# A conv stage whose TensorE instructions keep the order of the program, with tap products moved between projections, moments as column-tiled products and idle products

## The chip, the cores and the metric

The kernel runs on one core of a Trainium2 chip. The metric is the device time of one execution in microseconds (us), the median of several runs; one further execution was taken by the hardware profiler, and all rows below come from it. The engines are PE (TensorE; PEld is its weight load), DVE (VectorE), ACT (ScalarE), POOL (GpSimd) and SP (the queue that issues the DMAs). Each engine works through its own queue of instructions in order; semaphores make one wait for another.

## The reference

A decoder trunk of four layers on 256 tokens of 1024 channels. Every layer has a token mixer (latent attention, a Conformer convolution, a gated linear recurrence, attention again), a SwiGLU feed-forward part, and an embedding of its own that is gated by the residual stream. The change touches the convolution, layer 1:

```python
def _conformer_conv(u, w_pw1, b_pw1, w_dw, b_dw, ln_g, ln_b, w_pw2, b_pw2):
    a = u @ w_pw1 + b_pw1
    a = a[..., :CONV_CH] * jax.nn.sigmoid(a[..., CONV_CH:])
    a = lax.conv_general_dilated(a, w_dw[:, None, :].astype(a.dtype), window_strides=(1,),
                                 padding=[(CONV_WIDTH - 1, 0)],
                                 dimension_numbers=('NWC', 'WIO', 'NWC'),
                                 feature_group_count=CONV_CH) + b_dw
    a = jax.nn.silu(_layernorm(a, ln_g, ln_b))
    return a @ w_pw2 + b_pw2
```

That is: a projection to 2048 columns, a gate (GLU), a causal convolution of 31 taps for each of the 1024 channels by itself, a LayerNorm over the channels, silu, and an output product. Before it stands an RMSNorm of the residual, after it the residual is added.

## The kernel before, in words

All 256 tokens stay on the chip, as two tiles of 128 (the residual h); weights stream in. A large product is made of three (mm, L185): weight and activation are each split into a high and a low part, and high x high, high x low and low x high are added up in PSUM. The split of a weight is done by granule (L156): a DMA brings 128x1024 numbers (raw, 4 buffers), ACT rounds the high part (whi, 9 buffers, L167) and DVE subtracts for the low part (wlo, 8 buffers, L168).

In the conv stage channels lie on partitions, tokens on the free axis, and the 1024 channels are eight groups c of 128. Its steps, in the code's order:

- embed(1) (L387): 24 products of the layer's embedding, put into two PSUM banks ("mm") in turn, and copied to pph by ACT (L399). Then PE transposes the normed residual (hg to xT, L223).
- For each pair of groups the weights of conv_head are split, and for each group 48 products of 128x256 go to a bank of "acc" (4 buffers). ACT takes the sigmoid (L762), DVE the gated product glu (L766). For groups that are convolved on PE, tap weights tapw are loaded (L726, 2 buffers), and spread (L715) copies glu by four DMAs to four shifted windows (win, L722, 3 buffers).
- Groups 2 and 3 (CHAINS) are convolved on DVE, 31 steps each (L785, L787). The other six are convolved on PE by taps_pe (L728): 32 float32 products each, of 32 columns of weights, four of which take the four column quarters of the array.
- Groups 0 and 1 (BASE) come first. Their mean over channels (L775, weights self.mean, 1/1024 everywhere) gives base (L777), which is subtracted from all eight groups (L779, L792, L796), so that the variance can be computed as a mean of squares.
- moments (L742): for each group and token tile, co and its square (ACT, L740) are the weights of a product with two columns of self.mean, four products a group, all added up in one bank (stat) that puts the tokens on partitions. A product of ones with zeros opens that sum, another closes it (L713, L801).
- From the sums come variance, reciprocal root and mean (DVE, L803 to L808); they are put on diagonals (dg, L813) and broadcast over the partitions by PE (L814). The 24 products of embed(2) stand beside this. Then each group is normed (L822, L823), goes through silu (L824), is split and multiplied by w_pw2 (linear_rows, called at L829).

A scheduler decides in which order the instructions of one engine are issued: it takes the program's order as a start and moves instructions by the times at which it thinks their inputs are ready. issue_after and the list fence hold single instructions back. Buffers of a pool are reused in turn, so the load of a new weight waits until the split of an older one has read its buffer.

## Time and profile before

| what | time |
|---|---|
| three runs | 1421.79, 1421.91 and 1424.2 us |
| median | 1421.91 us |
| the profiled execution | 1418.08 us |
| its span (first to last instruction) | 1416.3 us |
| mean granted TensorE clock | 0.986 |

Rows of the profile are read like this. A window "A:B length, PE busy (x) ..." gives for each engine how long it worked between A and B (us from the span's start) and, in brackets, with how many instructions; then the clock that TensorE was granted (1.00 is full speed), the busy share of the DMA engines and their rate in GB/s. A row of the timeline has start, length, engine, line of the code, operation, output<-inputs, shapes and count; in square brackets, how long the engine sat idle before, and what ended that. A row of the chain of waits is one piece of the chain of work that ended last. A float32 matmul leaves two records, a matmul of fp32r numbers one. In the rows of instructions grouped by line, the last columns are busy time, mean ns of one, and idle time before them with what ended it.

### The profile page before, as it was taken

How to read it: one execution, taken by the hardware profiler on the slowest of the kernel's cores; microseconds unless marked ns; L12 is line 12 of the kernel's file. 1: busy time of each engine (PE TensorE's matmuls, PEld its weight loads, DVE VectorE, ACT ScalarE, POOL GpSimd, SP SyncE). 2: the span in 40 equal slices, each digit the busy share in tenths (PEclk: the TensorE clock that was granted, in tenths of full speed). 3: DMA queues.
4: the chain of work that ended last, by engine and by line, in shares of the span. 5: the costliest groups of instructions: out<-in, count | busy, mean ns of one | idle time of the engine just before them, and what ended most of it. 6: DMA issues, size and time to landing. Idle time of an engine off the chain costs nothing.

```text
span 1416.3 us, 20148 instructions
## 1 busy us (share of the span) xinstructions
PE 1368.3 (97%) x7269; PEld 1120.7 (79%) x7269; DVE 897.8 (63%) x1718; ACT 702.0 (50%) x1161; POOL 24.9 (2%) x55
## 2 busy tenths in 40 slices
PE   6999999998999999999999999999999999999996
PEld 6787788876976778887778887888878887788885
DVE  7866555558692965554877767555568867555556
ACT  6665444445521754443564445544445755444443
POOL 0100000000000000000000000000000100000000
PEclk9999999999897999999999999999999999999999
DMA  7523666636762466663564443755544623666632
GB/s 238 181 90 110 203 194 192 186 116 219 234 204 78 146 199 190 194 192 121 184 203 134 142 134 121 240 188 180 179 151 149 203 69 112 206 192 192 191 119 75
DMA packets 176326, 235.56 MB, mean 166 GB/s; under 512 B 11841, under 2 KB 139489, under 8 KB 176225
## 3 DMA queue, kind: packets, MB, share of 16 engines
q1 hardware_dynamic: 176224, 234.26, 52.5%
q8 instruction: 57, 0.93, 0.3%
q14 instruction: 45, 0.36, 0.1%
HBM read 229.68 MB, written 1.05 MB: 163 GB/s over the span
## 4 chain that ended last, share of the span: by engine, by line
PE 73%; DMA 9%; DVE 9%; ACT 5%; issue 3%; SPq 0%; DVEq 0%; ACTq 0%
PE mm L188 13%; PE mm L189 13%; PE mm L190 13%; PE acc L189 7%; PE acc L188 7%; PE acc L190 7%; DVE wlo L168 4%; DMA raw<-in_ffn_w_down_dram 4%; PE tr L223 3%; ACT whi L167 3%; DMA raw<-in_ple_w_gate_dram 2%; DVE co L787 1%; PE mm L732 1%; PE acc L949 1%; PE acc L619 1%
## 5 line engine op out<-in xcount | busy, mean ns | idle before, releaser
L168 DVE TENSOR_TENSOR wlo<-raw,whi 128x1024 fp32r<-128x1024 f32 (+2 forms) x420 | 498.8, 1201 | 153.5 <-ACT whi L167 110.5
L167 ACT ACTIVATE whi<-raw 128x1024 fp32r<-128x1024 f32 (+2 forms) x420 | 427.9, 1040 | 273.4 <-DMA raw<-in_ffn_w_down_dram 95.8
L188 PE MATMUL mm<-whi,xT 128*128 128x512 f32 x816 | 328.4, 402 | 0.7 <-ACT xT L210 0.4
L189 PE MATMUL mm<-wlo,xT 128*128 128x512 f32 x816 | 321.6, 394 | 0.0
L190 PE MATMUL mm<-whi,xT 128*128 128x512 f32 x816 | 321.5, 394 | 0.0
L190 PEld LDWEIGHTS mm<-whi,xT 128*128 128x128 f32 x816 | 153.3, 188 | 32.6 <-DVE xT L211 0.8
L188 PEld LDWEIGHTS mm<-whi,xT 128*128 128x128 f32 x816 | 153.5, 188 | 30.5 <-ACT xT L210 0.9
L189 PEld LDWEIGHTS mm<-wlo,xT 128*128 128x128 f32 x816 | 153.7, 188 | 28.4
L188 PE MATMUL acc<-whi,aT 128*128 128x512 f32 x352 | 138.6, 394 | 0.3
L189 PE MATMUL acc<-wlo,aT 128*128 128x512 f32 x352 | 138.7, 394 | 0.0
L190 PE MATMUL acc<-whi,aT 128*128 128x512 f32 x352 | 136.4, 389 | 0.0
L337 DVE SCALAR_TENSOR_TENSOR ga<-mm,rs_y,sg 128x256 f32<-128x256 f32 x88 | 42.4, 481 | 142.9 <-ACT sg L335 142.9
L335 ACT ACTIVATE sg<-mm,rs_y 128x256 f32<-128x256 f32 x88 | 40.9, 465 | 139.3 <-PE mm L190 139.2
L188 PE MATMUL acc<-whi,xT 128*128 128x512 f32 (+2 forms) x272 | 102.5, 379 | 1.4 <-ACT whi L167 0.8
L190 PE MATMUL acc<-whi,xT 128*128 128x512 f32 (+2 forms) x272 | 102.9, 380 | 0.2 <-DVE xT L211 0.2
L189 PE MATMUL acc<-wlo,xT 128*128 128x512 f32 (+2 forms) x272 | 102.5, 378 | 0.0
L188 PEld LDWEIGHTS acc<-whi,aT 128*128 128x128 f32 x352 | 66.1, 188 | 17.1 <-ACT aT L210 2.8
L190 PEld LDWEIGHTS acc<-whi,aT 128*128 128x128 f32 x352 | 66.1, 188 | 15.8 <-DVE aT L211 1.0
L189 PEld LDWEIGHTS acc<-wlo,aT 128*128 128x128 f32 x352 | 66.2, 188 | 13.0
L211 DVE TENSOR_TENSOR aT<-tr,aT 128x256 fp32r<-128x256 f32 x88 | 37.3, 423 | 53.3 <-ACT aT L210 53.3
L188 PEld LDWEIGHTS acc<-whi,xT 128*128 128x128 f32 x272 | 51.1, 189 | 10.3 <-ACT xT L210 1.3
L190 PEld LDWEIGHTS acc<-whi,xT 128*128 128x128 f32 x272 | 51.2, 188 | 8.3 <-DVE xT L211 0.8
(256 smaller groups left out, 1804.6 us busy)
## 6 DMA issues: line engine op xcount, KB each, us to landing
raw<-in_ffn_w_gu_dram SPq DMA_DIRECT2D x352, 256.0 KB, 4.4
raw<-in_ffn_w_down_dram SPq DMA_DIRECT2D x88, 512.0 KB, 4.4
raw<-in_ple_w_gate_dram SPq DMA_DIRECT2D x32, 512.0 KB, 4.9
raw<-in_hgrn_w_in_dram SPq DMA_DIRECT2D x64, 256.0 KB, 3.8
raw<-in_mla_w_out_dram SPq DMA_DIRECT2D x16, 512.0 KB, 4.2
raw<-in_conv_w_pw_dram SPq DMA_DIRECT2D x32, 256.0 KB, 5.0
raw<-in_mla_w_in_dram SPq DMA_DIRECT2D x16, 336.0 KB, 4.0
raw<-in_mla_w_uq_dram SPq DMA_DIRECT2D x12, 384.0 KB, 4.0
```

Of the source, the lines that this page charges most:

```text
L167: nc.scalar.activation(hi[:, :used], raw[:, :used], AF.Copy)
L168: nc.vector.tensor_tensor(out=lo[:, :used], in0=raw[:, :used], in1=hi[:, :used].bitcast(F32), op=ALU.subtract)
L188: mm(ps, x[0], w[0], start=start, stop=False)
L189: mm(ps, x[0], w[1], start=False, stop=False)
L190: return mm(ps, x[1], w[0], start=False, stop=stop)
L211: v = self.nc.vector.tensor_tensor(out=lo, in0=src, in1=hi.bitcast(F32), op=ALU.subtract)
L223: nc.tensor.transpose(pt[:, (i - k0) * P : (i - k0 + 1) * P], src[:, i * P : (i + 1) * P], self.ident)
L335: nc.scalar.activation(sg, ps[:, :256], AF.Silu, scale=r)
L337: nc.vector.scalar_tensor_tensor(out=ga, in0=ps[:, 256:], scalar=r, in1=sg, op0=ALU.mult, op1=ALU.mult)
L619: nc.tensor.matmul(s1[:, hh], qT[:HD, h, P:], kT[:HD, h], start=True, stop=False)
L732: nc.tensor.matmul(ps[32 * j : 32 * j + 32], tapw[c][:, j, m], win[c][:, j, QUAD * m : QUAD * m + S], start=m == 0, stop=m == STEPS - 1,)
L787: V.scalar_tensor_tensor(out=co[:, c], in0=xin[c][:, k : k + S], scalar=par(c, k), in1=co[:, c], op0=ALU.mult, op1=ALU.add)
```

## The change

It rewrites the conv stage's order and three of its steps. While self.pinned is set, every matmul that goes through the new helper is issued in the order of the program. Groups 0 and 1 are now those convolved on DVE, their chains begin behind the gate of group 2 and advance six taps with each further group; groups 2 and 3 make the base. The taps of a group follow the projection that is two groups later, and load the tap weights of the group after next when they are issued. The moments are column-tiled: for each pair of groups four products with 32 columns of self.mean as weights and co or its square, 256 tokens, as moving input, one for each column quarter; the sums lie on four rows, are copied to SBUF, and two products with a matrix select put them on the tokens' partitions. embed(1) takes the four banks of "acc"; behind it come 12 bf16 products that nobody reads. The buffers called "work" go from five to three, and the squares have four of their own ("sq").

```diff
+    def matmul(self, *args, **kw):
+
+        ins = self.nc.tensor.matmul(*args, **kw)
+        if self.pinned:
+            self.tc.keep_in_program_order(ins)
+        return ins
...
-        mm = self.nc.tensor.matmul
+        mm = self.matmul
...
+    def idle(self, n):
+
+        ps = self.bank("mm", 2)[:, :S]
+        for _ in range(n):
+            self.matmul(ps, self.ident_bf, self.causal.rearrange("p h n -> p (h n)"), start=True, stop=True)
+
+    def embed(self, i, bank=None):
...
-                ps = self.bank("mm", 2)
+                ps = bank() if bank else self.bank("mm", 2)
...
+        self.select = C.tile([P, 2], F32, name="select")
+        nc.gpsimd.memset(self.select, 0.0)
+        for j in range(QUAD):
+            nc.gpsimd.memset(self.select[32 * j : 32 * j + 1, j % 2 : j % 2 + 1], 1.0)
...
-        BASE = 2
-        CHAINS = (2, 3)
+        CHAINS, BASE = (0, 1), (2, 3)
...
-            self.embed(i)
+            self.embed(i, self.acc)
+            self.idle(12)
...
-            zero = tmp("zero", [P, 4 * NT], 1)
-            nc.gpsimd.memset(zero, 0.0)
-            stat = self.bank("tr", 2)
-            nc.tensor.matmul(stat[:, : 4 * NT], self.ones, zero, start=True, stop=False)
-            xin, win, tapw, sq = [], {}, {}, {}
+            xin, win, tapw, sq = {}, {}, {}, {}
...
-                        nc.tensor.matmul(
+                        self.matmul(
...
-                return ps
+                if c + 2 < KD:
+                    tap_weights(c + 2)
+                if c in BASE:
+                    nc.scalar.activation(co[:, c], ps, AF.Identity, bias=par(c, TAPS))
+                else:
+                    V.scalar_tensor_tensor(out=co[:, c], in0=ps, scalar=par(c, TAPS), in1=self.base, op0=ALU.add, op1=ALU.subtract)
+                    square(c)
 
             def square(c):
-                sq[c] = tmp("work", [P, S], 5)
-                return nc.scalar.activation(sq[c], co[:, c], AF.Square)
...
+                sq[c] = tmp("sq", [P, S], 4)
+                self.sq = nc.scalar.activation(sq[c], co[:, c], AF.Square)
+
+            stats = []
+
+            def moments(pair, last=False):
+
+                if not stats:
+                    stats.append(self.bank("tr", 2)[:, :S])
+                first = len(stats) == 1
+                stats.append(pair)
+                for q, c in enumerate(pair):
+                    for m, x in enumerate((co[:, c], sq[c])):
+                        j = 2 * q + m
+                        ins = self.matmul(stats[0][32 * j : 32 * j + 32], self.mean[:, :32], x, start=first, stop=last)
+                return ins
...
+            def chain(c, k0, k1):
+                for k in range(k0, k1):
...
+            def set_base():
+
+                pm = self.bank("tr", 2)[:, :S]
+                for b in BASE:
+                    self.matmul(pm, self.mean, co[:, b], start=b == BASE[0], stop=b == BASE[-1])
+                self.base = tmp("base", [P, S], 1)
+                V.tensor_scalar(out=self.base, in0=pm, scalar1=KD / len(BASE), scalar2=None, op0=ALU.mult)
+                for c in BASE:
+                    V.tensor_tensor(out=co[:, c], in0=co[:, c], in1=self.base, op=ALU.subtract)
+                    square(c)
+
+            self.pinned = True
+            for c in (2, 3):
+                tap_weights(c)
+            for c in range(KD):
...
+                if c not in CHAINS:
+                    spread(c)
+                if c == 4:
+                    taps_pe(2)
+                if c == 5:
+                    taps_pe(3)
+                if c == 6:
+                    set_base()
+                    taps_pe(4)
+                if c >= 2:
+                    k = min(TAPS, 6 * (c - 1))
+                    for b in CHAINS:
+                        chain(b, 6 * (c - 2), k)
+            taps_pe(5)
+            moments(BASE)
             self.embed_weights(2)
             rows = lambda k: self.granule([(a["conv_w_pw2"][0][k * P : (k + 1) * P], 0)], 1, D)
             ws = [rows(k) for k in range(5)]
-            for c in CHAINS:
-                V.tensor_tensor(out=co[:, c], in0=co[:, c], in1=base, op=ALU.subtract)
-                square(c)
-                moments(c)
-            for c in range(4, KD):
-                V.scalar_tensor_tensor(out=co[:, c], in0=taps_pe(c), scalar=par(c, TAPS), in1=base, op0=ALU.add, op1=ALU.subtract)
-                fence = [square(c).ins]
-                fence.append(moments(c).ins)
+            taps_pe(6)
+            moments((4, 5))
+            for b in CHAINS:
+                V.tensor_tensor(out=co[:, b], in0=co[:, b], in1=self.base, op=ALU.subtract)
+                square(b)
+            taps_pe(7)
+            fence = [self.sq.ins]
+            moments(CHAINS)
+            fence.append(moments((6, 7), True).ins)
...
-            nc.tensor.matmul(stat[:, : 4 * NT], self.ones, zero, start=False, stop=True)
+            sums = tmp("sq", [P, S], 4)
+            V.tensor_copy(sums, stats[0])
+            tok = self.bank("tr", 2)
+            for t in range(NT):
+                self.matmul(tok[:, 2 * t : 2 * t + 2], sums[:, t * P : (t + 1) * P], self.select, start=True, stop=True)
             st = tmp("st", [P, 2, NT], 1)
-            V.tensor_copy(st, stat[:, : 4 * NT].rearrange("p (m t two) -> p m t two", m=2, two=2)[:, :, :, 0])
+            V.tensor_copy(st, tok[:, : 2 * NT].rearrange("p (t m) -> p m t", m=2))
...
+            self.pinned = False
```

The order in which the instructions are issued changes at three places on which much of the stage hangs. In the rows, a number behind a name tells one buffer's use from another's; xN stands for N like rows in a line.

TensorE, in the stage's end. Before, here is where the taps of group 4 (mm_4257) and the moments of groups 0 to 2 are (tr_3478 is the bank of the sums, work the squares):

```order
L732 MATMUL mm_4257<-win_3827,tapw_3770 32x256 x17
L748 MATMUL tr_3478<-mean,co_3475 128x2
L732 MATMUL mm_4257<-win_3827,tapw_3770 32x256 x8
L748 MATMUL tr_3478<-mean,work_4120 128x2
L748 MATMUL tr_3478<-mean,co_3475 128x2
L748 MATMUL tr_3478<-mean,work_4120 128x2
L748 MATMUL tr_3478<-mean,co_3475 128x2
L732 MATMUL mm_4257<-win_3827,tapw_3770 32x256 x4
L748 MATMUL tr_3478<-mean,work_4127 128x2
L748 MATMUL tr_3478<-mean,co_3475 128x2
L748 MATMUL tr_3478<-mean,work_4127 128x2
L748 MATMUL tr_3478<-mean,co_3475 128x2
```

After, this is all from the last product of group 7's projection (acc_4174) to group 7's taps (mm_4373; mm_4236 are those of group 5, mm_4327 of group 6, tr_4274 the bank of the sums):

```order
L188 MATMUL acc_4174<-xT_3248,wlo_4047 128x256
L188 MATMUL mm_4236<-win_3972,tapw_4010 32x256 x32
L188 MATMUL tr_4274<-co_3494,mean 32x256
L188 MATMUL tr_4274<-sq_4119,mean 32x256
L188 MATMUL tr_4274<-co_3494,mean 32x256
L188 MATMUL tr_4274<-sq_4122,mean 32x256
L188 MATMUL mm_4327<-win_4108,tapw_4157 32x256 x32
L188 MATMUL tr_4274<-co_3494,mean 32x256
L188 MATMUL tr_4274<-sq_4160,mean 32x256
L188 MATMUL tr_4274<-co_3494,mean 32x256
L188 MATMUL tr_4274<-sq_4272,mean 32x256
L188 MATMUL mm_4373<-win_4229,tapw_4269 32x256 x32
```

The moments stand in fours between whole groups of taps, where they were strewn among them one by one; group 7's taps have nothing but moments, statistics and embedding products behind them.

The queue SP, from group 6's to group 7's windows. Before (win_4047 and win_4109 are those of groups 6 and 7, tapw_3990 and tapw_4052 their tap weights):

```order
L722 DMA win_4047<-glu_4043 128x1x284 x4
L164 DMA raw_4233<-in_conv_w_pw_dram 128x1024
L164 DMA raw_4239<-in_conv_w_pw_dram 128x1024
L164 DMA raw_4512<-in_conv_w_pw_dram 128x1024
L164 DMA raw_4530<-in_conv_w_pw_dram 128x1024
L726 DMA tapw_3990<-in_conv_taps_dram 128x1024
L722 DMA win_4109<-glu_4105 128x1x284 x4
L726 DMA tapw_4052<-in_conv_taps_dram 128x1024
L164 DMA raw_4548<-in_conv_w_pw_dram 128x1024
L164 DMA raw_4691<-in_ffn_w_gu_dram 128x2x256 x2
```

After (win_4108 and win_4229 are those of groups 6 and 7, tapw_4157 and tapw_4269 their tap weights):

```order
L736 DMA win_4108<-glu_4104 128x1x284 x4
L165 DMA raw_4323<-in_conv_w_pw_dram 128x1024
L740 DMA tapw_4157<-in_conv_taps_dram 128x1024
L165 DMA raw_4516<-in_conv_w_pw_dram 128x1024
L165 DMA raw_4534<-in_conv_w_pw_dram 128x1024
L165 DMA raw_4552<-in_conv_w_pw_dram 128x1024
L736 DMA win_4229<-glu_4225 128x1x284 x4
L740 DMA tapw_4269<-in_conv_taps_dram 128x1024
L165 DMA raw_4695<-in_ffn_w_gu_dram 128x2x256 x2
```

Tap weights of a group now stand behind taps that ran before, and four loads of 128x1024 stand between the windows of group 6 and those of group 7.

VectorE, between the gates of groups 6 and 7. Before (glu_4043 and glu_4105 are those gates):

```order
L766 SCALAR_TENSOR_TENSOR glu_4043<-acc_3992,cb_1806,work_4041 128x256
L787 SCALAR_TENSOR_TENSOR co_3475<-glu_3738,cpar,co_3475 128x256
L168 TENSOR_TENSOR wlo_4208<-raw_4209,whi_4207 128x1024
L787 SCALAR_TENSOR_TENSOR co_3475<-glu_3738,cpar,co_3475 128x256
L168 TENSOR_TENSOR wlo_4214<-raw_4215,whi_4213 128x1024
L168 TENSOR_TENSOR wlo_4220<-raw_4221,whi_4219 128x1024
L168 TENSOR_TENSOR wlo_4226<-raw_4227,whi_4225 128x1024
L766 SCALAR_TENSOR_TENSOR glu_4105<-acc_4054,cb_1806,work_4103 128x256
L777 TENSOR_SCALAR base_4117<-tr_4114 128x256
L779 TENSOR_TENSOR co_3475<-co_3475,base_4117 128x256 x2
```

After (glu_4104 and glu_4225 are those gates; base_4116 is the base):

```order
L809 SCALAR_TENSOR_TENSOR glu_4104<-acc_4053,cb_1806,work_4102 128x256
L789 TENSOR_SCALAR base_4116<-tr_4113 128x256
L791 TENSOR_TENSOR co_3494<-co_3494,base_4116 128x256 x2
L169 TENSOR_TENSOR wlo_4304<-raw_4305,whi_4303 128x1024
L831 TENSOR_TENSOR co_3494<-co_3494,base_4116 128x256 x2
L755 SCALAR_TENSOR_TENSOR co_3494<-mm_4124,cpar,base_4116 128x256
L169 TENSOR_TENSOR wlo_4310<-raw_4311,whi_4309 128x1024
L169 TENSOR_TENSOR wlo_4316<-raw_4317,whi_4315 128x1024
L169 TENSOR_TENSOR wlo_4322<-raw_4323,whi_4321 128x1024
L809 SCALAR_TENSOR_TENSOR glu_4225<-acc_4174,cb_1806,work_4223 128x256
L755 SCALAR_TENSOR_TENSOR co_3494<-mm_4236,cpar,base_4116 128x256
```

Four low parts of weights, the base and the subtractions stand between the two gates, and the last three low parts right ahead of group 7's.

More of the change, by code (lines that the diff above doesn't have):

```diff
@@ L735, in taps_pe @@
                         )
-                return ps
-            def square(c):
-                sq[c] = tmp("work", [P, S], 5)
-                return nc.scalar.activation(sq[c], co[:, c], AF.Square)
-            def moments(c):
-                for t in range(NT):
-                    s = slice(t * P, (t + 1) * P)
-                    for m, x in enumerate((co[:, c, s], sq[c][:, s])):
-                        at = 2 * (NT * m + t)
-                        last = nc.tensor.matmul(stat[:, at : at + 2], x, self.mean[:, :2], start=False, stop=False)
-                return last
@@ L751, in conv @@
-            for c0 in range(0, KD, 2):
-                ws = self.conv_head(i, c0) if c0 else self.head
-                for cc in range(2):
-                    c = c0 + cc
-                    if c not in CHAINS:
-                        tap_weights(c)
-                    ps = self.acc()
-                    for half in range(2):
-                        s = slice(half * 256 + cc * P, half * 256 + (cc + 1) * P)
-                        self.mms(ps[:, half * S : (half + 1) * S], [(hi[:, s], lo[:, s]) for hi, lo in ws], xs)
-                    sg = tmp("work", [P, S], 5)
-                    nc.scalar.activation(sg, ps[:, S:], AF.Sigmoid, bias=self.cb1[:, KD + c : KD + c + 1])
-                    x = tmp("glu", [P, PAD + S + 2], 4)
-                    nc.gpsimd.memset(x[:, :PAD], 0.0)
-                    nc.gpsimd.memset(x[:, PAD + S :], 0.0)
-                    V.scalar_tensor_tensor(out=x[:, PAD : PAD + S], in0=ps[:, :S], scalar=self.cb1[:, c : c + 1], in1=sg, op0=ALU.add, op1=ALU.mult)
-                    xin.append(x)
-                    if c not in CHAINS:
-                        spread(c)
-                if c0 == 4:
-                    for c in range(BASE):
-                        nc.scalar.activation(co[:, c], taps_pe(c), AF.Identity, bias=par(c, TAPS))
@@ L787, in conv @@
                         V.scalar_tensor_tensor(out=co[:, c], in0=xin[c][:, k : k + S], scalar=par(c, k), in1=co[:, c], op0=ALU.mult, op1=ALU.add)
+            def set_base():
[11 more added lines that the diff above has]
+            for c in range(KD):
+                if c % 2 == 0:
+                    ws = self.conv_head(i, c) if c else self.head
+                ps = self.acc()
+                for half in range(2):
+                    s = slice(half * 256 + c % 2 * P, half * 256 + (c % 2 + 1) * P)
+                    self.mms(ps[:, half * S : (half + 1) * S], [(hi[:, s], lo[:, s]) for hi, lo in ws], xs)
+                sg = tmp("work", [P, S], 3)
+                nc.scalar.activation(sg, ps[:, S:], AF.Sigmoid, bias=self.cb1[:, KD + c : KD + c + 1])
+                x = xin[c] = tmp("glu", [P, PAD + S + 2], 4)
+                nc.gpsimd.memset(x[:, :PAD], 0.0)
+                nc.gpsimd.memset(x[:, PAD + S :], 0.0)
+                V.scalar_tensor_tensor(out=x[:, PAD : PAD + S], in0=ps[:, :S], scalar=self.cb1[:, c : c + 1], in1=sg, op0=ALU.add, op1=ALU.mult)
+                if c not in CHAINS:
[13 more added lines that the diff above has]
+            moments(BASE)
             self.embed_weights(2)
@@ L814, in conv @@
                     nc.tensor.matmul(bc[:, m, t], self.ones, dg, start=True, stop=True)
+            self.pinned = False
             self.fence = fence + [last.ins]
@@ L820, in conv @@
             for c in range(KD):
-                z = tmp("work", [P, S], 5)
+                z = tmp("work", [P, S], 3)
                 V.tensor_tensor(out=z, in0=co[:, c], in1=rb, op=ALU.mult)
```

12 lines of the change are left out of this document (removed).

## The prediction

> **What bounds the kernel now.** I read the page first, its busy times and its row of the granted clock in 40 slices.
>
> ```profile
> PE 1368.3 (97%) x7269; PEld 1120.7 (79%) x7269; DVE 897.8 (63%) x1718; ACT 702.0 (50%) x1161; POOL 24.9 (2%) x55
> ```
>
> ```profile
> PEclk9999999999897999999999999999999999999999
> ```
>
> TensorE is busy for 97% of the span (1416.3 us), so time goes only where its work shrinks, its clock rises or a wait of its own ends. The clock row dips in slices 11 and 13 (354 to 389 us and 425 to 460 us), which is the conv stage, all that the change touches. So I cut that stage by granted clock in the view of windows.
>
> ```profile
> core 0: us, PE busy (x) PEld busy (x) DVE busy (x) ACT busy (x) POOL busy (x), PEclk, DMA share, GB/s
> 354.84:365.08 10.24, 8.44 (x36) 7.30 (x35) 8.49 (x12) 5.78 (x8) 2.35 (x1) 0.50 0.79 247
> 365.08:423.11 58.03, 54.91 (x546) 49.77 (x544) 45.97 (x90) 20.58 (x27) 0.62 (x8) 1.00 0.70 210
> 423.11:440.17 17.06, 17.02 (x112) 11.40 (x110) 2.84 (x3) 2.72 (x7) 0.00 (x0) 0.50 0.33 105
> 440.17:453.83 13.66, 12.61 (x175) 7.83 (x168) 1.78 (x6) 2.74 (x5) 0.00 (x0) 1.00 0.34 118
> 453.83:457.24 3.41, 3.41 (x10) 2.67 (x9) 2.71 (x17) 0.60 (x1) 0.00 (x0) 0.50 0.00 0
> ```
>
> The projections run at full clock. Then come 17.06 us in which taps and moments are computed at half clock, and 3.41 us more at the stage's end. The timeline of PE shows what stands ahead of the first (idle time and its releaser in brackets); the chain of waits (start, length, what) shows what runs inside it and after it.
>
> ```profile
> 421.96 0.38 PE L748 MATMUL tr<-mean,co 128*128 128x2 f32 x2 [3.12 <-DVE co L779]
> ```
>
> ```profile
> 423.49 1.87 PE tr L748 x8
> ...
> 442.72 0.76 PE tr L748 x6
> ```
>
> A float32 product leaves two records (the tap row below has 128 for the 64 products of two groups), so a moment product takes 0.47 us there (four in 1.87) and 0.25 at full clock (three in 0.76). The sum below forecasts the start of the first product of linear_rows, which ends the stage (461.94 us, with the tail's rows below). What follows it is left alone, and its weights lie ready: from 453.83 on no DMA runs.
>
> **The change part by part.** At 365.08 the clock is full and group 0 half projected. What PE does from there I add up anew, from windows of PE alone over the two stretches of projections, and a window of the tap products alone, which lies between them.
>
> ```profile
> 365.08:396.87 31.79, 31.79 (x266) 1.00 0.77 230
> 403.92:415.66 11.74, 11.74 (x101) 1.00 0.53 142
> ```
>
> ```profile
> 396.87:403.92 7.05, 7.05 (x128) 4.06 (x128) 1.00 0.41 111
> ```
>
> The projections are the same 384 products in both kernels; those left at 365.08 take 31.79 + 11.74 = 43.5 us. Taps are computed on PE for six groups in both; two take 7.05, so six 21.2 us (0.11 us for each column-tiled product of 256 tokens). Of the moments, 32 products of two columns (32 x 0.25 = 8.0 us at full clock, twice that at half) become 16 of the shape of a tap product. I take a tap product's time, 16 x 0.11 = 1.8 us. The lower end can't be under that, since each streams the same 256 columns; the upper is a 128-wide float32 product of 256 tokens, the mean sum in this row of the timeline (four records, two products, 1.02 us, so 0.5 us each and 8.0 in all), should the four not run beside each other.
>
> ```profile
> 415.54 1.02 PE L775 MATMUL tr<-co,mean 128*128 128x256 f32 x4
> ```
>
> The mean sum keeps its 1.0 us and moves ahead of the taps of group 4. Its wait for the activation of group 3's taps is hidden by the 5.8 us of group 6's projection (48 x 0.12). The sum is 365.1 + 43.5 + 21.2 + 1.8 + 1.0 = 432.6 us, if PE never waits. Counted back from there, group 6 is projected at 410.0, group 7 at 420.2, and group 7's taps are due at 428.2 (432.6 less 3.5 of taps and 0.9 of moments).
>
> The wait that is added is that for group 7's last transfers. Its windows and tap weights are the last loads of the stage, and PE, whose order is now fixed, can't do anything else meanwhile: behind these taps stand eight moment products, the statistics and the output product.
>
> ```profile
> 413.70 2.64 SPq L722 DMA_DIRECT2D win<-glu  x4
> ```
>
> ```profile
> raw<-in_conv_w_pw_dram SPq DMA_DIRECT2D x6, 512.0 KB, 5.7
> ```
>
> ```profile
> DMA to landing us min/median/max: 3.8/4.3/7.4
> ```
>
> ```profile
> 419.36 0.47 ACT work L762
> ...
> 420.63 0.48 DVE glu L766
> ```
>
> These are the issue of a group's windows on SP (timeline), the landing of the weight loads around it (issues from 411 to 428 us), that of the tap weights, and group 7's sigmoid and glu in the chain. In the new order group 7's glu stands on VectorE behind three low parts of weights, the last one's load behind group 6's windows. Group 6 projected at 410.0, sigmoid and glu 1.0, four window issues 2.6, landing of the load 5.7, its high part 1.0 and low part 1.2 (means of the page's rows below): 421.5. That is later than the sigmoid of group 7 itself (420.7). With glu 0.5, its window issues 2.6 and the tap weights behind them on the same queue (4.3 to land), it is 428.9 when they are there, 0.7 after PE is due; with the longest landing, 7.4, 3.8 after. As three loads of 512 KB stand right ahead on the queue, I take about the middle, 2.4 us, and keep both ends.
>
> The 24 products of embed(1), now with four banks, no longer wait for pph, which the second of these pieces shows:
>
> ```profile
> 346.60 0.40 PE L188 MATMUL mm<-whi,pT 128*128 128x512 f32 x1
> 346.84 0.40 PE L189 MATMUL mm<-wlo,pT 128*128 128x512 f32 x1
> ```
>
> ```profile
> 353.60 0.51 PE L188 MATMUL mm<-whi,pT 128*128 128x512 f32 x1 [1.97 <-ACT pph L399]
> ...
> 357.29 1.08 PE L223 MATMUL tr<-ident,hg 128*128 128x128 f32 x4 [1.77 <-DVE hg L78]
> ```
>
> At 0.23 us apart they end at 346.6 + 24 x 0.23 = 352.1. The 12 that nobody reads cost 12 x 0.11 = 1.3 us at a tap product's rate for 256 columns (0.5 each and 6 us if they went like the mean sum) and end at 353.4. The transposes wait for hg, that is VectorE and the loads, until 357.29. So both change nothing; without that cover the idle products would cost their 1.3 us.
>
> What drops the clock stands in three more windows; the piece of the chain behind them is a projection product at half clock.
>
> ```profile
> 351.42:354.84 3.42, 1.45 (x6) 1.05 (x6) 1.86 (x5) 2.83 (x4) 0.00 (x0) 1.00 1.01 337
> 419.69:423.11 3.42, 1.15 (x18) 0.71 (x18) 3.18 (x7) 1.17 (x3) 0.00 (x0) 1.00 0.98 335
> 730.30:733.70 3.40, 1.64 (x10) 1.13 (x9) 2.18 (x3) 3.35 (x6) 0.00 (x0) 1.00 0.97 307
> ```
>
> ```profile
> 364.06 0.21 PE acc L190
> ```
>
> After 3.4 us with 42% and 34% of PE busy it was halved, with 48% not. The pause before the transposes, 353.4 to 357.3, still leaves a stretch of that kind, so I keep the half clock up to 365.08 as it was. [...] I charge one stretch at half clock, 3.4 / 2 = 1.7 us; the ends are 0 and 3.4.
>
> [...]
>
> The tail, from the last moment product to linear_rows, is in the chain of waits
>
> ```profile
> 453.40 0.33 PE mm L188
> ...
> 461.94 0.50 PE acc L188
> ```
>
> ```profile
> 421.03 0.41 DVE L777 TENSOR_SCALAR base<-tr 128x256 f32<-128x256 f32 x1
> ```
>
> 461.94 - 453.40 = 8.5 us, by way of VectorE's statistics. There come on top the copy of the sums (0.4, as base in the second row), two select products (0.25 each, the two-column rate) and up to three embedding products ahead of them (0.3 by what they outlast the copy): 9.7 us. At full clock the embedding products among the chain leave up to 1.0 less than this, since the broadcasts stand behind them; should the added products come at half clock, their 0.8 doubles.
>
> On VectorE the chains of groups 0 and 1 now begin with group 2, ahead of low parts of weights. From its timeline:
>
> ```profile
> 370.65 0.48 DVE L766 SCALAR_TENSOR_TENSOR glu<-acc,cb,work 128x256 f32<-128x256 f32 x1 [5.18 <-ACT work L762]
> ...
> 398.70 12.37 DVE L787 SCALAR_TENSOR_TENSOR co<-glu,cpar,co 128x256 f32<-128x256 f32 x31
> ```
>
> ```profile
> L168 DVE TENSOR_TENSOR wlo<-raw,whi 128x1024 fp32r<-128x1024 f32 (+2 forms) x420 | 498.8, 1201 | 153.5 <-ACT whi L167 110.5
> L167 ACT ACTIVATE whi<-raw 128x1024 fp32r<-128x1024 f32 (+2 forms) x420 | 427.9, 1040 | 273.4 <-DMA raw<-in_ffn_w_down_dram 95.8
> ```
>
> Between the first glu and the last low part for groups 6 and 7 stand 48 chain steps (0.40 each), five glu (0.48) and eight low parts (1.2): 370.7 + 19.2 + 2.4 + 9.6 = 401.9. Group 6's first products come at 404.2 (410.0 less 5.8), so this costs nothing with 2.3 us in hand. The 31 taps on two groups are the same work as before; fewer "work" and more "sq" buffers, the other memsets and the subtraction of base from other groups change neither count nor path. Tap weights for groups 4 to 6 are issued over 10 us before their use, against 4.3 to land.
>
> **Sum.** 432.6 + 2.4 + 1.7 + 9.7 = 446.4 against 461.9: 15.5 us less. The profiled execution took 1418.08 us (1.8 around its span), so 1402.6; the median of the runs, 1421.91, is 3.8 above it, and I carry the difference over to it: 1406.4. As a check by what goes: the wait of 3.1, half of 17.1, the moments' 6.2 and some 1.5 us of small waits are 19.3; 2.4, 1.7 and 1.2 come back, which leaves 14.0.
>
> **The rivals.** The clock holds (chance 0.15): a wait short of 1.9 us doesn't halve it, and the idle products fill enough of the pause before the transposes. Then 1.7 goes, the wait is nearer 0.7 (1.7), and at the start 24 projection products take 0.12 in place of 0.21 us (2.2 more): 1401 us. [...] The moments don't run side by side (0.08), so that the change does not do what it says there: 16 x 0.5 in place of 1.8 adds 6.2: 1412.6. Against it stands the tap row, the same tiling. VectorE comes late (0.17): it runs in order, so a chain step that waits for a glu, or a low part that waits for its load, holds all behind it, group 7's glu last. In the old kernel that glu came at 420.63, 5.0 us after the projections' end (415.66), held up by a low part. It costs nothing up to 2.3 us of delay and then one for one. Up to 12.7 us beyond it the change is still faster (0.08, some 1412); to 18.3 it can't be told from none (0.05, about 1422). Only from 18 us on, where nearly every low part waits for a load of 5.7 us and three such waits add up, is it slower (0.04): some 1427.
>
> **How the numbers follow.** The forecast has 0.60. Its own range comes from the wait (0.7 to 3.8), the clock (0 to 3.4) and the tail (8.7 to 10.5): 1402 to 1410. The range is 1399.5 to 1414, down to the held clock with the short tail, up to the untiled moments and the mild lateness. A measurement of this kernel can tell about 0.2%, 2.8 us. Faster by more: 0.60 + 0.15 + 0.08 + 0.08 = 0.91; within: 0.05; slower: 0.04.
>
> **What would show it.** In the new profile the first product of linear_rows starts near 446 us, and PE goes from group 7's projection to its taps with 1 to 4 us of idle before them and nowhere else. The granted clock is 1.00 from 365 to about 428 us, and the moment products take 0.11 us. The forecast is wrong if the projections wait for low parts (groups 4 to 7 longer than 5.8 us each), if a clock of 0.50 shows earlier, or if a stage after linear_rows waits where it did not.

## The result, and the profile after

The changed kernel takes 1401.65 us in the median of four runs (1400.18 to 1402.87), the kernel before 1421.85 in the median of its four by then (1419.49 to 1424.2): 20.2 us less, a ratio of 0.9846 with a 95% interval of 0.9821 to 0.987. The profiled execution of the changed kernel took 1402.87 us.

The page of the profile after, its span, busy times and clock:

```profile
span 1400.9 us, 20099 instructions
...
PE 1351.1 (96%) x7249; PEld 1109.8 (79%) x7249; DVE 898.1 (64%) x1719; ACT 700.4 (50%) x1161; POOL 26.2 (2%) x59
...
PEclk9999999999999999999999999999999999999998
```

VectorE and ScalarE do the same work as before, TensorE is busy for 17 us less, and the dip of the clock in slices 11 and 13 is gone. The windows of the conv stage, cut by granted clock and with the columns of before, show what is left of it:

```profile
359.39:362.80 3.41, 3.29 (x15) 3.03 (x15) 2.06 (x3) 2.85 (x4) 2.37 (x1) 0.50 0.78 255
362.80:431.07 68.27, 65.28 (x720) 56.28 (x722) 52.98 (x98) 26.39 (x37) 0.70 (x8) 1.00 0.77 240
431.07:434.48 3.41, 3.41 (x36) 2.16 (x39) 0.00 (x0) 0.00 (x0) 0.00 (x0) 0.50 0.13 44
434.48:446.68 12.20, 11.07 (x89) 7.60 (x81) 6.70 (x29) 5.14 (x10) 0.00 (x0) 1.00 0.01 1
```

6.8 us at half clock, where there were 30.7 (10.24 + 17.06 + 3.41). From group 7's projection on, the timeline of PE has two waits, one of 2.99 us ahead of group 7's taps and one of 0.99 ahead of linear_rows; the chain of waits shows what ends the first:

```profile
420.02 3.66 PE L188 MATMUL mm<-win,tapw 128*32 128x256 f32 x64
430.99 5.35 PE L188 MATMUL mm<-win,tapw 128*32 128x256 f32 x64 [2.99 <-DMA tapw<-in_conv_taps_dram]
446.68 0.50 PE L188 MATMUL acc<-whi,xT 128*128 128x512 f32 x1 [0.99 <-ACT xT L218]
```

```profile
420.79 0.04 ACT whi L168
...
421.75 0.47 ACT work L805
...
423.02 0.49 DVE glu L809
...
426.13 0.02 SPq L740
...
426.18 4.68 DMA tapw<-in_conv_taps_dram
430.85 0.14 issue
430.99 5.35 PE mm L188 x64
436.33 1.66 PE tr L188 x16
```

Group 7's sigmoid (L805) comes behind a high part of weights (L168), its glu at 423.02, then its windows, then its tap weights, and PE stands still from 428.0 to 431.0. Linear_rows starts at 446.68, and from there to the end it is 954.2 us, as before (954.4).

Executions of one kernel differ in layer 0 already: the transposes of layer 0's gate start at 331.18 us in the first profile of the changed kernel and at 329.27 in its second. So stages are compared from here on by one stretch, from the transposes of layer 0's gate (329.96 in the first row, before; 331.18 after) to the first product of linear_rows:

```profile
329.96 1.23 PE L223 MATMUL tr<-ident,hg 128*128 128x128 f32 x8 [0.97 <-DVE hg L69]
```

```profile
331.18 1.23 PE L231 MATMUL tr<-ident,hg 128*128 128x128 f32 x8 [1.72 <-DVE hg L69]
```

It fell from 132.0 us (461.94 - 329.96) to 115.5. The table has it for every run, read from the same two rows of each trace, with the longest wait of PE between the last projection and the last taps, and the time at half clock in the stage's two ends. The kernel before had medians of 1420.9 to 1422.1 us beside these runs, which were made on more than one chip. Two slow executions are left out of the medians and ratios: one of tapw7_early (2229.09 us at a granted clock of 0.557) and one of before beside all_idle22 (1676.74 us at 0.75).

| run | median us | ratio to before (95%) | stretch us | wait us | half clock at the start, at the end, us |
|---|---|---|---|---|---|
| before, 1st profile | 1421.85 | | 132.0 | 3.1 | 10.2, 20.5 |
| before_2 (2nd profile) | | | 131.8 | 3.1 | 6.8, 20.5 |
| changed | 1401.65 | 0.9846 (0.9821 to 0.987) | 115.5 | 3.0 | 3.4, 3.4 |
| same | 1400.49 | 0.9846 (0.9818 to 0.9874) | 113.9 | 2.5 | 3.4, 0 |
| unpinned | 1401.6 | 0.9851 (0.9822 to 0.988) | 115.7 | 3.4 | 3.4, 3.4 |
| old_moments | 1404.13 | 0.9869 (0.9845 to 0.9894) | 118.0 | 0 | 3.4, 6.8 |
| before_tiled | 1406.97 | 0.9895 (0.9867 to 0.9923) | 118.7 | 4.4 | 0, 6.8 |
| before_early | 1415.09 | 0.9962 (0.9944 to 0.998) | 128.0 | 2.2 | 0, 17.1 |
| idle0 | 1404.03 | 0.9882 (0.9851 to 0.9913) | 113.4 | 1.7 | 6.8, 0 |
| idle40 | 1404.16 | 0.9881 (0.985 to 0.9912) | 116.8 | 3.7 | 0, 6.8 |
| early_glu | 1400.12 | 0.9848 (0.9821 to 0.9874) | 114.0 | 2.4 | 6.8, 0 |
| tapw7 | 1397.86 | 0.9845 (0.9816 to 0.9875) | 111.6 | 0.5 | 3.4, 0 |
| tapw7_early | 1394.98 | 0.9823 (0.9794 to 0.9852) | 110.8 | 0 | 3.4, 0 |
| all_idle22 | 1397.76 | 0.9841 (0.9821 to 0.9862) | 110.9 | 0 | 3.4, 0 |

### The profile page after: what moved, and what is told of

It is laid out like the page before. It is cut to its first block, busy times and chain, and to the rows that moved or that the text cites. A ratio compares the mean times of both kernels' runs of the same rounds, so it can differ in the third digit from the quotient of the medians.

```text
span 1400.9 us, 20099 instructions
## 1 busy us (share of the span) xinstructions
PE 1351.1 (96%) x7249; PEld 1109.8 (79%) x7249; DVE 898.1 (64%) x1719; ACT 700.4 (50%) x1161; POOL 26.2 (2%) x59
## 4 chain that ended last, share of the span: by engine, by line
PE 78%; DMA 8%; DVE 6%; ACT 5%; issue 3%; SPq 1%; DVEq 0%; ACTq 0%
PE mm L188 42%; PE acc L188 25%; PE tr L231 4%; ACT whi L168 2%; DVE wlo L169 2%; DMA raw<-in_ffn_w_down_dram 2%; DMA raw<-in_ple_w_gate_dram 2%; DMA raw<-in_mla_w_ukv_dram 1%; PE acc L992 1%; PE acc L633 1%; DMA raw<-in_conv_w_pw_dram 1%; DMA raw<-in_hgrn_w_in_dram 1%; PE tr L614 1%; PE tr L654 1%; PE acc L659 1%
## 5 line engine op out<-in xcount | busy, mean ns | idle before, releaser
L168 ACT ACTIVATE whi<-raw 128x1024 fp32r<-128x1024 f32 (+2 forms) x420 | 427.8, 1040 | 265.3 <-DMA raw<-in_ffn_w_down_dram 99.2
L188 PE MATMUL mm<-whi,xT 128*128 128x512 f32 x1632 | 546.7, 398 | 0.8 <-ACT xT L218 0.4
L188 PE MATMUL acc<-whi,aT 128*128 128x512 f32 x704 | 232.9, 392 | 0.7 <-DVE aT L219 0.6
L188 PE MATMUL acc<-whi,xT 128*128 128x512 f32 (+2 forms) x544 | 165.4, 380 | 1.7 <-ACT xT L218 1.4
L218 ACT ACTIVATE xT<-tr 128x512 fp32r<-128x512 f32 (+1 forms) x72 | 37.5, 526 | 40.5 <-PE tr L231 39.7
L188 PEld LDWEIGHTS acc<-wlo,xT 128*128 128x128 f32 x272 | 51.5, 190 | 7.8
L188 PE MATMUL mm<-whi,cT 128*128 128x384 f32 (+1 forms) x160 | 52.3, 382 | 4.4 <-ACT q L602 4.1
L218 ACT ACTIVATE aT<-tr 128x256 fp32r<-128x256 f32 x88 | 33.0, 375 | 46.2 <-PE tr L231 46.0
L231 PE MATMUL tr<-ident,hg 128*128 128x128 f32 x192 | 31.2, 288 | 22.6 <-DVE hg L69 16.5
L70 ACT ACTIVATE junk<-h 128x512 bf16<-128x512 f32 x48 | 30.0, 626 | 45.1 <-DVE h L320 25.7
```

The costliest lines, as they stand in the source:

```text
L70: square = nc.scalar.activation(T.tmp("junk", [P, 512], 1, BF16), h[:, s], AF.Square, accum_out=ss[:, c : c + 1])
L168: nc.scalar.activation(hi[:, :used], raw[:, :used], AF.Copy)
L188: ins = self.nc.tensor.matmul(*args, **kw)
L218: a = self.nc.scalar.activation(hi, src, AF.Copy)
L231: nc.tensor.transpose(pt[:, (i - k0) * P : (i - k0 + 1) * P], src[:, i * P : (i + 1) * P], self.ident)
```

## Experiments: what the gain is made of

**same** is the changed kernel once more.

> The changed kernel again, as a measure for the runs beside it. The sum of the prediction gives 15 to 16 us less than before (ratio 0.989); the runs so far gave 20 us (0.985). If the sum holds, more runs come nearer to 0.989 and a profile again shows the first product of linear_rows near 446.5 us; if something outside the conv stage also gained, the ratio stays at 0.985 and some later stage is shorter than before.

Its median is 21.6 us under that of before, its profile has the stretch at 113.9 us: 1.6 less than the first profile, with no half clock behind a wait of 2.5 us. The first product of linear_rows started at 443.1. So the part that was expected of the sum alone (a ratio of 0.989) didn't come, and no later stage is shorter either: 954.5 us from linear_rows on.

**before_2** is the kernel before, for a second profile.

> The kernel before once more, for a second profile. Its first profile was of an execution 4 us under its median (1418.1 against 1422), that of the changed kernel at its median, and that is the difference between the 15 us of the sum and the 20 us of the medians. If the excess lies in the conv stage: the stretch from the gate's transposes of layer 0 (329.96 us in the first profile) to the first product of linear_rows (461.94) is longer than 132.0 us here, with more stretches at half clock or a longer wait for group 7's glu, by about what the time is above 1418. If it lies elsewhere: 132 us again, whatever the time.

It took 1418.02 us, and the stretch is 131.8 us with the same wait and the same 17.1 us at half clock. Both profiled executions of before so took 1418 us, where the medians of its runs lie at 1421 to 1422 and single ones between 1414 and 1429. The traces show 16 to 18 us of gain in the stage; where the 3 to 4 us are by which the medians lie above them, no trace shows.

**old_moments** puts back the old moments, and nothing else:

```diff
-                        ins = self.matmul(stats[0][32 * j : 32 * j + 32], self.mean[:, :32], x, start=first, stop=last)
+                            ins = self.matmul(stats[0][:, at : at + 2], x, self.mean[:, :2], start=False, stop=False)
...
-            V.tensor_copy(sums, stats[0])
...
-                self.matmul(tok[:, 2 * t : 2 * t + 2], sums[:, t * P : (t + 1) * P], self.select, start=True, stop=True)
+            self.matmul(stats[0][:, : 4 * NT], self.ones, zero, start=False, stop=True)
```

> The changed kernel with the moments as before (four products of two columns for each group, opened and closed by the products of ones and zeros), at the changed places. Theory of the sum: 32 x 0.25 in place of 16 x 0.11 us adds 6.2, the copy and the two select products go (1.2): 5 us slower than the changed kernel, up to 8 if the last sixteen fall into the half clock. Rival, that the new places of the taps carry the gain and the moments lie beside other work: within 1 us of the changed kernel.

2.5 to 3.6 us slower than the changed kernel's two medians; the stretch is 2.5 to 4.1 us longer. That lies between the two theories, as each had left out one thing. The moments do take longer, but group 7's loads arrive meanwhile: PE doesn't wait at all. And what they cost is paid in the clock, in these windows of PE's last taps, the last sixteen moments (from 434.0 on) and the tail:

```profile
430.20:433.59 3.39, 3.28 (x61) 2.39 (x65) 0.00 (x0) 0.00 (x0) 0.00 (x0) 1.00 0.11 39
433.59:437.00 3.41, 3.41 (x39) 3.00 (x28) 0.48 (x1) 1.90 (x3) 0.00 (x0) 1.00 0.02 5
437.00:443.83 6.83, 6.83 (x21) 5.70 (x21) 3.02 (x19) 0.60 (x1) 0.00 (x0) 0.50 0.00 0
```

In the second window PE is busy for every one of its 3.41 us, and yet the clock is halved behind it. All but its first 0.4 us is filled with products of two columns.

**before_tiled** is the other half alone: the kernel before with the new moments, copy and select products (moments by pairs; diff as above, the other way round).

> The kernel before with the column-tiled moments, copy and select products alone; places of the taps, chains, base and embedding as before. Theory of the sum: the half clock behind the late glu stays, 20 moments at 0.47 and 12 at 0.25 us (12.4) become 16 at up to 0.22 (3.5), 1.2 come back in the tail and about 1 in a wait for the last tap weights: 6 to 8 us faster than before. Rival (the new places carry it): 0 to 2 us faster.

15.1 us faster than before, twice what was expected, and neither theory gave it. The stretch is 13.3 us shorter, though the late glu of group 7 still makes PE wait, even longer than before (4.4 us against 3.1). Up to 2.9 of the 13.3 us are luck at the stage's start, of which the edit touches only the one product that opened the old sum: the clock was not halved there this time (nor in before_early, which leaves that product), and the last product of the projections starts 82.5 us behind the gate's transposes, where it started 85.5 us behind them in the first profile of before and 85.3 in the second. From there on the stage is 10.4 us shorter. Windows ahead of, within and behind its half clock:

```profile
415.26:418.67 3.41, 1.29 (x21) 0.48 (x10) 2.29 (x3) 1.82 (x3) 0.00 (x0) 1.00 0.88 290
418.67:425.50 6.83, 4.43 (x34) 1.77 (x36) 5.37 (x9) 3.34 (x7) 0.00 (x0) 0.50 0.86 307
425.50:438.81 13.31, 13.09 (x220) 8.61 (x214) 1.69 (x4) 1.25 (x3) 0.00 (x0) 1.00 0.60 195
```

Here too a half clock comes with the wait (416.6 to 420.9 us), but it ends after 6.83 us; with two-column products among the taps it took 17.06 us, PE busy for 17.02 of them. The second dip, in the tail, is gone too. The expectation had charged only the moments' own time, and had kept the half clock.

**before_early** was to take most of the wait out of the kernel before, and leaves its moments:

```diff
+            self.fence = [gate.ins, glu.ins]
             ws = [rows(k) for k in range(5)]
+            self.fence = []
```

(gate and glu are group 7's sigmoid and glu; behind the fence stand the high and low parts of w_pw2.)

> The kernel before with the splits of w_pw2's weights held behind group 7's sigmoid and glu; moments and places as before. This takes most of the 3.1 us wait away but leaves the two-column moments. If these count little for the clock (in the run with the old moments at the changed places it fell at 437.0 with no wait ahead of it): the 17 us at half clock stay, or come elsewhere among the moments, and it is 2 to 5 us faster than before. If the wait alone brings the half clock: 3.1 + 8.5, that is 10 to 12 us faster.

5.8 us faster in the medians, the stretch 4.0 us shorter. Again up to 2.7 us of that are luck, as the clock was not halved at the start; from the last product of the projections on the stage is 1.3 us shorter. The wait itself only fell from 3.1 to 2.2 us, since chain steps and low parts on VectorE still stand ahead of group 7's glu and the base, and PE was busy for 35% of the stretch in which it lies. So this run does not show what the kernel before would do without the wait. The time at half clock at the stage's end is again 17.1 us, now in two pieces; ahead of the second PE was busy for 82% of a stretch (2.80 of 3.40 us):

```profile
414.20:417.60 3.40, 1.18 (x12) 0.46 (x10) 3.37 (x7) 1.81 (x3) 0.00 (x0) 1.00 0.89 246
417.60:427.80 10.20, 10.20 (x82) 6.04 (x82) 6.50 (x8) 4.21 (x7) 0.00 (x0) 0.50 0.66 215
431.30:434.70 3.40, 2.80 (x28) 1.76 (x27) 0.48 (x1) 0.42 (x1) 0.00 (x0) 1.00 0.10 11
434.70:441.50 6.80, 6.80 (x56) 3.66 (x58) 0.00 (x0) 0.00 (x0) 0.00 (x0) 0.50 0.92 316
```

Ahead of the second piece PE had waited for 0.6 us only, so the reading that the wait alone brings the half clock doesn't hold for this piece. Nor does the busy share of PE tell where it comes: the clock was halved behind stretches of about 3.4 us with 0% (idle0, below), 34%, 42% and 79% (before), 63% (all_idle22, below) and 100% of PE busy (old_moments), and not behind one with 48% (before, the prediction's third row). What halves it these runs don't show. Nor does a run tell what it is about the old moments: they differ from the new ones in the two moving columns and in the 128 columns of weights that each of them loads. The row of before with 79%, ahead of the half clock of 3.41 us at its stage's end, is

```profile
450.41:453.83 3.42, 2.70 (x27) 1.95 (x20) 0.81 (x4) 1.90 (x3) 0.00 (x0) 1.00 0.00 0
```

New moments alone give 13.3 us of the stretch, the new places alone 14.0 (old_moments against before), both together 16.5 to 18.1, each with some luck at the start in it. Either one alone takes the half clock at the stage's end from 20.5 to 6.8 us, so that they don't add up.

**unpinned** leaves the order to the scheduler:

```diff
-            self.pinned = True
+            self.pinned = False
```

> The changed kernel with the scheduler left free to order TensorE's instructions. One product of group 1's projection moves ahead by 45 places, some chain steps of VectorE trade places; nothing else does. If the gain comes from the order in which the code is written: as the changed kernel, within 0.2%. If holding the scheduler to it matters (the one product waits for a bank, or the chain steps hold up low parts): 1 to 3 us slower.

1401.6 us against 1401.65 and 1400.49, the stretch 115.7. The order comes from the place of the lines in the code; holding the scheduler to it changes nothing that can be measured.

## Experiments: the products nobody reads, and the wait that is left

**idle0** drops the call, **idle40** has 40 in place of 12.

```diff
-            self.idle(12)
```

> The changed kernel without the 12 products that nobody reads. Prediction's step (they lie beside the wait for VectorE and change nothing): within 1 us of the changed kernel. Rival (they keep the clock up): in all profiles of the changed kernel the clock was halved for one stretch of 3.4 us around the transposes, in the one of before for three; without them it is two or three again, 1.7 to 3.4 us slower, with a window of 0.50 from about 354 us on.

> The changed kernel with 40 such products in place of 12: they last 4.6 to 5.0 us and fill the wait of 3.5 to 3.8 us before the transposes nearly whole. If the clock follows how much PE does in a stretch of 3.4 us: no 0.50 around 360 us, the transposes and a dozen projection products at full clock, 1 to 2 us faster than the changed kernel. If they change nothing, as the prediction has it for the twelve: within 0.5 us. If they run past the wait: up to 1 us slower.

Without them the clock is halved for 6.82 us at the transposes in place of 3.41, behind a window in which PE did nothing:

```profile
352.65:356.06 3.41, 0.00 (x0) 0.00 (x0) 2.92 (x6) 2.79 (x5) 0.00 (x0) 1.00 0.71 240
356.06:362.88 6.82, 5.48 (x23) 4.98 (x24) 5.10 (x8) 4.25 (x6) 2.36 (x1) 0.50 0.84 253
```

Yet the stretch is 113.4 us, no longer than in any run of the changed kernel: the last product of the projections starts 0.3 to 0.9 us later than in the changed kernel's two profiles, and the wait before group 7's taps is 1.7 us in place of 2.5 and 3.0. With 40, 18 of which the scheduler put between and behind the transposes, the start has no half clock at all, and the projections end 1.0 to 1.5 us sooner, yet the stretch is 116.8: a wait of 3.7 us comes ahead of group 6's taps. On VectorE a low part of weights whose load landed late now stands ahead of group 6's glu, which comes at 417.46 us, where in the changed kernel it came at 411.71; so group 6's windows and tap weights are issued late. First the changed kernel, then the one with 40:

```profile
411.71 0.47 DVE L809 SCALAR_TENSOR_TENSOR glu<-acc,cb,work 128x256 f32<-128x256 f32 x1
```

```profile
416.31 1.23 DVE L169 TENSOR_TENSOR wlo<-raw,whi 128x1024 fp32r<-128x1024 f32 x1 [3.31 <-ACT whi L168]
417.46 0.48 DVE L809 SCALAR_TENSOR_TENSOR glu<-acc,cb,work 128x256 f32<-128x256 f32 x1
```

The medians of both are 2.4 to 3.7 us above those of the changed kernel, with intervals that overlap. So the traces show no worth in the twelve, and the medians don't exclude 3 us.

**early_glu** holds the splits of the last three weights behind group 7's gate, by a fence as in before_early.

> The changed kernel with the splits of the last three weights (high part on ScalarE, low part on VectorE) held behind group 7's sigmoid and glu. Theory: the wait of 3.0 us before group 7's taps comes from these splits, whose loads land late; the glu then comes near 421 in place of 423.0 us, the wait falls to 0.5 to 1.5 us, and the half clock behind it goes too: 1.5 to 4 us faster. Rival: the tap weights' landing alone ends the wait (their buffer comes free with group 5's taps): at most 0.7 us faster.

1400.12 us: no gain that can be told. Group 7's windows were issued from 420.73 on, 2.8 us sooner than in the changed kernel (1.5 sooner by the start of the stretch), and PE waited 2.4 us all the same. The queue SP, in the changed kernel and then here:

```profile
423.56 2.51 SPq L736 DMA_DIRECT2D win<-glu  x4
426.18 1.10 SPq L740 DMA_DIRECT2D tapw<-in_conv_taps_dram  x1
```

```profile
420.73 2.50 SPq L736 DMA_DIRECT2D win<-glu  x4
423.33 0.55 SPq L165 DMA_DIRECT2D raw<-in_conv_w_pw_dram  x1
423.97 0.42 SPq L740 DMA_DIRECT2D tapw<-in_conv_taps_dram  x1
```

From issue to landing the windows took up to 3.2 us here and the tap weights 5.7. So the windows were there by 425.8, before group 7's taps were due at 427.5, and the tap weights landed at 429.7: they alone end the wait, as the rival says. The buffer that the rival names was not what held their load when it was issued: group 5's taps had read it until 423.1, and the load came 0.9 us later, behind the windows and one more load; in the changed kernel it came 2.5 us behind those taps. But the buffer is the next limit. Issued at 423.1 and with the same 5.7 us to land, the tap weights would, as an estimate, still be 1.3 us late.

**tapw7** loads group 7's tap weights into a buffer of the weight loads (raw), so that it waits for no taps; the load is now issued at 414.23 us, ahead of group 7's windows. **tapw7_early** does both.

```diff
-                if c + 2 < KD:
+                if c + 2 < KD - 1:
...
+            raw = self.tmp("raw", [P, 1024], 4, pool=self.wpool)
+            nc.sync.dma_start(raw, a["conv_taps"][:, KD - 1].rearrange("p j m n -> p (j m n)"))
+            tapw[KD - 1] = raw.rearrange("p (j m n) -> p j m n", j=QUAD, m=STEPS)
             taps_pe(6)
```

> The changed kernel with group 7's tap weights in a buffer of the weight loads, so that their load needn't wait for group 5's taps; group 7's glu stays late. Theory, that two things end the wait before group 7's taps, glu with its windows and the tap weights' buffer, within 0.5 us of each other: the windows alone still hold it (last issue near 426, 4.6 us to land), so at most 0.5 us faster than the changed kernel. Rival, that the tap weights alone hold it: the wait of 2.5 to 3.0 us goes to 1 or less, and the half clock with it, 2 to 4 us faster.

> Both: tap weights of group 7 early, and the last splits held behind group 7's glu. Theory of two ends: the windows are issued by 423.3 and land near 427.8, group 7's taps are due at 427.5, the wait is 0.3 to 1 us, no half clock behind it; the stretch from the gate's transposes to linear_rows falls from 113.9 to 115.5 us (changed kernel) to 111.5 to 113, 1.5 to 3 us faster than the changed kernel. Rival, that something else is late next (moments' squares, the loads for linear_rows): no gain over the run with the early glu alone.

The first was expected to bring 0.5 us at most, and brought 2.6 to 3.8 in the medians, 2.3 to 3.9 in the stretch. Its ratio to the runs of before beside it, 0.9845, is that of the changed kernel (0.9846), so the times alone show no gain; the wait in the trace does. In its timeline and in that of the run with both, group 7's taps read:

```profile
426.37 4.51 PE L188 MATMUL mm<-win,raw 128*32 128x256 f32 x63 [0.49 <-PE tr L188]
```

```profile
424.80 3.64 PE L188 MATMUL mm<-win,raw 128*32 128x256 f32 x64
```

With the tap weights there, PE waits 0.5 us for the windows and 0.9 more among the taps, in which three weight loads wait for a window (0.7 us in all); of the 3 us the windows held 1.4, the tap weights the rest. With both, nothing waits there, and no half clock follows. Its median of 1394.98 us is the lowest of all runs, 5.5 to 6.7 us under those of the changed kernel; its ratio's interval (0.9794 to 0.9852) overlaps theirs, but the stretch, 110.8 us, is 3 to 5 us shorter, and the trace shows why.

**all_idle22** is that run with 22 of the products, all ahead of the transposes.

> The run with both repairs (group 7's tap weights early, splits behind its glu) and 22 products that nobody reads in place of 12; all 22 stand ahead of the transposes and last 2.6 us. If the clock follows how much PE does in a stretch: the half clock of 3.4 us at the transposes, which the run with both still had, goes, the first projections take 0.12 us from the start, and the stretch from the gate's transposes to linear_rows falls from 110.8 to 109.0 to 110.0 us; the median falls by 1 to 1.7 us to about 1394. If the twelve more or fewer are worth nothing, as their removal showed: the same as the run with both within 0.5 us.

The stretch is 110.9 us, and the half clock of 3.4 us at the transposes is still there. 22 products leave a pause of 2.2 us, and in the 3.41 us ahead of the half clock PE was busy for 63%:

```profile
355.07:358.48 3.41, 2.14 (x13) 1.52 (x14) 2.63 (x4) 1.81 (x3) 1.88 (x1) 1.00 0.88 292
```

The products are worth nothing here either: the median, 1397.76 us, is 2.8 us above that of the run with both, where 1 to 1.7 less was expected, with intervals that overlap. Of the two runs with both repairs this one lies 2.7 to 3.9 us under the changed kernel, so how much the repairs bring in the median is known only roughly.

## Why the prediction was right, and where not

The sum gave linear_rows a start at 446.4 us; it was 446.68. That it comes so near is in part luck. Counted from the gate's transposes the sum is 116.4 us, against 115.5, 113.9 and 115.7 in the three profiles of the changed kernel (unpinned with them). And within it the wait, the last taps and the last moments came out 1.3 us longer together, the tail 1.0 us shorter. By its terms:

- **Up to group 7's projection**: forecast 420.2, measured 420.1. Two things cancel. The forecast kept the 10.24 us at half clock at the transposes, there were 3.41 (some 1.3 us less, measured from the gate's transposes); and this execution was 1.2 us later in layer 0.
- **Taps and moments**: a group's taps take 3.59 us (forecast 3.53), four moment products 0.43 (0.44): chain of early_glu, where no wait disturbs them:

```profile
419.53 3.59 PE mm L188 x64
423.12 0.43 PE tr L188 x8
423.55 3.45 PE mm L188 x64
```

  The column quarters do run beside each other: in tapw7 the first records of four products start between 425.26 and 425.28 us, their second ones between 425.48 and 425.50, and each lasts 0.38 us. So that rival falls. The last eight take 1.66 in place of 0.9 us, at full clock too (same, early_glu): the last group's subtraction (0.48) and square (0.42) stand ahead of them. This wait was in the chain of before and was left out of the sum.
- **The wait that is added**: forecast 2.4 (0.7 to 3.8), measured 3.0, 2.5 and 3.4. Its place was right, and so was its chain: glu late behind the splits (423.0, forecast 421.5), then the windows, then the tap weights on the same queue (issued at 426.18, forecast 424.6; 4.7 us to land, forecast 4.3 to 7.4). The runs add what the sum had not asked: the tap weights' late place is worth about half of the wait (tapw7), an early glu alone nothing (early_glu).
- **Half clock behind it**: 1.7 charged, for 3.41 us at half clock; 5.35 - 3.59 = 1.8 in the first profile, nothing in the run same with its wait of 2.5 us. That the added wait brings this half clock, and that 1.9 us of waiting do, no run shows: the 1.7 was the author's estimate. In its place the runs showed 3.4 us at half clock behind waits of 3.0 (changed) and 3.4 us (unpinned) and none behind those of 2.5 (same), 2.4 (early_glu) and 1.7 us (idle0). The prediction read the busy share as what drops the clock; old_moments has it halved behind 3.41 us with PE busy throughout. That part of the change's worth was in the sum (the 17 us were counted at full clock), its cause was not.
- **Tail**: 8.7 (446.68 - 437.99), forecast 9.7 with 8.7 as the end at full clock; the clock was full.
- **VectorE's lateness**: the chains cost PE nothing. From 362.80 to 431.07 it is busy for 65.28 of 68.27 us, and the 2.99 that are missing are the wait for the tap weights. But the mean sum, whose wait for group 3's activation was held to be hidden by group 6's projection, waited for 0.7 us in same and 0.8 in tapw7_early, as ScalarE did that activation late.
- **Idle products and four banks**: no wait for pph is left, and the transposes wait for hg as forecast (3.8 us). The cover held.
- **From the profiled execution to the median**: here the forecast failed by 4.8 us of the 20. It added 3.8 us, by which the profiled execution of before lay under the median, to the changed kernel as well; the latter's profiled execution took 1402.87 us, forecast 1402.6, but is the slowest of its four. Both profiles of before lie 3 to 4 us under its medians. This isn't explained: their stretches are equal within 0.2 us, and no unprofiled execution has a trace. The measured median lies just under the range of the sum itself (1402 to 1410), and at the 1401 us of the rival that the clock holds; yet in this profile it did not hold: it was halved at the start and behind the wait. So the agreement with that rival's number is luck.

## What to carry to other kernels

The moment products of two moving columns were paid twice here: in their own time (0.25 us each at full clock, where four of the new ones take 0.43), and in the clock of the work that is mixed with them (20.5 us at half clock at the stage's end in before, 6.8 in before_tiled). Where other kernels have such products, this is worth a look. Where an order is fixed, look for all that the last load needs, its place on the queue, what stands ahead of it, and its buffer: of two ends that lie near each other, taking away the earlier one shows nothing (early_glu). And before a difference is carried from a profile to a median, look how far the profiled execution lies from the runs.

## What the runs showed that was not expected

The clock fell behind a stretch of 3.41 us in which PE was busy throughout, with two-column products (old_moments at 437.0), and it came back after 6.8 us behind a longer wait (4.4 us against 3.1) once the same sums were made of 256-column products (before_tiled), where it took 17.1 with two-column ones. And in the changed kernel, taking away a half clock at the start of the stage, or adding one, didn't show in the stage's length (idle0 with 6.8 us: 113.4; same with 3.4: 113.9). Group 7's loads end the wait at the end whatever PE gained before: in changed, same, unpinned, idle0 and early_glu group 7's taps start 99.4 to 100.0 us behind the gate's transposes. In the kernel before, the projections end 2.5 to 2.9 us sooner without a half clock at the start (before_tiled and before_early against the two profiles of before), and how much of that remains at the stage's end is not separated.
